# A decoder layer on one core: running sum folded to 64 rows, three places reordered, last stores in halves

## Chip, cores and metric

One core of a Trainium2 chip runs the whole kernel. The metric is device time in microseconds (us) of the execution. The kernel before took 849.17 us in the median of three runs (848.13 to 849.51).

## The reference

One layer of a hybrid causal decoder in fp32, for 512 tokens of width 1024:

```python
h = rms_norm(x, norm_mix)
q_a, k_a, v_a, u_b, gate_b, gate_c, g_a, g_b = split(h @ w_in)
o_a = stick_breaking_attention(heads(q_a), heads(k_a), heads(v_a))   # 8 heads of 64
y_b = gate_b * causal_depthwise_conv(gate_c * u_b, conv_w)           # 3 taps, 512 channels
merged = sigmoid(g_a) * (o_a @ w_branch_a) + sigmoid(g_b) * (y_b @ w_branch_b)
x = x + merged @ w_mix_out
x = x + memory_cross_attention(rms_norm(x, norm_mem_q), rms_norm(mem, norm_mem_kv), ...)  # 256 memory tokens
gate, up = split(rms_norm(x, norm_ffn) @ w_ffn_in)                   # 2816 hidden channels
x = x + (silu(gate) * up) @ w_ffn_out
return rms_norm(x, norm_final)
```

In the stick-breaking attention the weight of key s for query t, with scores z, is

```python
log_fail = where(mask, log_sigmoid(-z), 0)
log_later = cumsum(log_fail, reverse) - log_fail     # the sum over keys between s and t
weights = where(mask, exp(log_sigmoid(z) + log_later), 0)
```

## The kernel before

Activations lie with channels on the 128 partitions and the 512 tokens along the free axis. To hold fp32 precision every operand of a product is kept as two parts, hi (a cast to the matmul's fp32r type, on ScalarE) and lo (the rest, a subtract on VectorE), and a product is three matmuls, hi·hi, lo·hi and hi·lo (`mm3`, L154 to L156). Weights come in tiles of 128x1024, four buffers deep, and are split in the same way (L149, L150).

The stages, by the profiled execution: values of the attention (to 27 us), the stick-breaking stage (27 to 195), branches and merging (to 304), memory keys and values (to 348), the mixing projection with its residual (to 401), memory attention and its output projection (to 508), feed-forward input (508 to 731), feed-forward output (to 840), final norm and stores (to 847).

**The stick-breaking stage.** Four pairs of heads (p = 0 to 3), and in each the four key blocks of 128 keys from the last (kt = 3) to the first (kt = 0): 16 steps. Block kt has 512 − 128·kt queries. For kt of 3 and 2 both heads of a pair share one tile, for 1 and 0 each head has its own. In each step:

- `scores` (L437) makes z in one of four PSUM banks. ScalarE takes |z|, exp and log (L444 to L446), VectorE adds max(z, 0) (L447), GpSimd applies the causal mask (L402). That is e, minus the log of the chance to fail.
- `fails` splits e into the two parts l (L416, L417), and adds the running sum of the later key blocks into e (L462). It is queued in `urgent`.
- `rests` splits this sum into the two parts r (L416, L417 again). It is queued in `behind`, and so runs right after `fails` in the same settling. There are three of them in a pair: the one of kt = 3 is the split l itself, the one of kt = 2 is one 128x512 tile, the ones of kt = 1 are two 128x384 tiles.
- `weights` adds onto z the sum over the keys: a matmul with a matrix of −1 for each part of the rest (L480) and one with a triangle of −1 for each part of l (L483). ScalarE takes exp (a, L485), GpSimd masks (L402), VectorE scales and splits into ah and al (L489, L490).
- `values` multiplies by the values (L502).

Between these steps stand the projections of the coming pair, the convolution (gc L372, cu L378, L379, its taps cv L359, L363, gb L387) and two gates, so that TensorE always has a gemm to run. Here the framework's scheduler places instructions on the engines by the order in which the code issues them and by their dependences. `settle_behind`, called once a step, empties the two queues. At step 9 the factors of the memory's norm go by two GpSimd DMAs to DRAM and back (rmd L534, rmb L536).

**After it.** The merged tiles m = 0 to 7 are split as soon as each is made (mh, ml, L172 and L174); the memory keys km follow (products L154 to L156, eviction L642).

**Feed-forward input.** Seven products for each of 22 blocks m of hidden channels ("forms" i = 0 to 6, L855) in the order of the list `uses`; forms 0, 3, 4 and 5 share PSUM bank z of their block, 2 and 6 bank y. `reads` and `second` take intermediate sums out of the banks: sa on ScalarE (L876), fg and sb on VectorE (L878, L881, L886). The weight forms wf are made six uses ahead (L844, L845). The mean of the norm (acch, accl, L184, L185) is split at use (1,1). The order of TensorE, ScalarE and VectorE is written out by hand in this region and up to the end.

**End.** The last product is made in two halves of 256 columns (`last_half`, p5b L1317). The squares' sum of the last half goes to s1b by ScalarE's accumulator (L1321), VectorE adds it to the other two sums (L1279), ScalarE takes log and exp (L1283, L1284), VectorE corrects (L1293, L1298), and the last two tiles are scaled and stored, 128x512 each, one by the queue of SyncE (SP) and one by that of ScalarE (L1304, L1306, L1309).

Of the kernel before, what the change touches and what calls it, by code (L numbers as in the profile page):

```python
# [13 lines left out]
P = 128  # L14
# [29 lines left out]
def hybrid_layer(ctx: ExitStack, tc: tile.TileContext, xT_d, memT_d, mem_d, cols_d, wv_d, win_d,  # L44
# [28 lines left out]
    def f(ap):  # L73
        return ap.bitcast(F32)
# [224 lines left out]

    urgent, behind = [], []  # L300

    def settle_behind(*last):
        while urgent or behind:
            (urgent or behind).pop(0)(*last)

# [114 lines left out]
    def rests(p, kt, hs, e, w, last):  # L420
        rest[p, kt - 1, hs] = lsplit(e, w, f"r{kt}", 4 // len(hs), last)

# [29 lines left out]
    def fails(p, kt, hs, e, n, last):  # L452
        w = len(hs) * n
        sp[p, kt, hs] = lsplit(e, w, f"l{kt}", 4 // len(hs), last)
        if kt == TT - 1:
            later[hs] = e
            rest[p, kt - 1, hs] = sp[p, kt, hs]
        elif kt > 0:
            t = by_head(e, n)[:, :, P:]
            before = heads_of(kt + 1)[0] if len(heads_of(kt + 1)) == 1 else hs  # L460
            old = by_head(part_of([later[before]], before, hs, n - P)[0], n - P)
            nc.vector.tensor_tensor(out=t, in0=t, in1=old, op=ALU.add)  # L462
            later[hs] = e
            behind.append(lambda *last: rests(p, kt, hs, e, w, last))

# [146 lines left out]
    for m in range(KD):  # L612
# [24 lines left out]
    for m in range(KD):  # L637
# [413 lines left out]
    with tc.manual_schedule(engines={mybir.EngineType.PE, mybir.EngineType.Activation,  # L1051
# [6 lines left out]
        for n, (m, i) in enumerate(uses):  # L1058
# [6 lines left out]
            else:  # L1065
                if i == 1 and m > 0:
                    second(m - 1)
# [206 lines left out]
        def rstd(ts):  # L1274


            a, b = ss[:, :TT][:, ts], ss[:, TT:][:, ts]
            if ts == t1:
                nc.vector.tensor_scalar(out=var[:, ts], in0=b, scalar1=a, scalar2=s1b, op0=ALU.add,  # L1279
                                        op1=ALU.add)  # L1280
            else:
                nc.vector.tensor_tensor(out=var[:, ts], in0=a, in1=b, op=ALU.add)
            after(nc.scalar.activation(ry[:, ts], var[:, ts], AF.Ln, bias=eps_t), tables)  # L1283
# [17 lines left out]
        def store(t, h, how):  # L1301
# [6 lines left out]
            q = nc.scalar if (t, h) == (1, 0) else nc.sync  # L1308
            q.dma_start(out[t * P:(t + 1) * P, h * 512:(h + 1) * 512], y)  # L1309

# [26 lines left out]
        half()  # L1337
        store(0, 0, "act")
        half = last_half(1)
# [70 lines left out]
```

## Time and profile before

| | before |
|---|---|
| median of three runs | 849.17 us (848.13 to 849.51) |
| profiled execution | 848.86 us |
| its span | 847.2 us, granted TensorE clock 0.998 |
| PE (TensorE) busy | 837.0 us, 99% |
| DVE (VectorE) busy | 654.0 us, 77% |
| ACT (ScalarE) busy | 453.3 us, 54% |
| POOL (GpSimd) busy | 158.9 us, 19% |
| DMA | 143.72 MB, mean 170 GB/s |

The profiled execution's own time is 1.7 us above its span, and 0.3 below the median. In a row of a timeline stand the start in us, the busy time, engine, line, operation, out<-in by the program's names without numbers, tile sizes and types, the count if neighbouring instructions are merged into one row, and in brackets the idle time before it with what ended it. Rows of one engine overlap by up to some tenths, since an instruction's drain lies under the next one's start: the pitch from start to start says what an instruction costs its engine. In the table of waits stand the total, the number of waits and the longest. A row of a window has its length, then the busy time and instruction count of each engine, the TensorE clock, the DMA share and GB/s.

### The profile page before, as it was taken

Reading aid. Unit: us, or ns where it says so; the run is one execution under the profiler, and the core shown is the slowest. Engines: PE = TensorE matmul, PEld = TensorE weight load, DVE = VectorE, ACT = ScalarE, POOL = GpSimd, SP = SyncE. Lnnn points to the kernel's source line nnn. Section 1 sums busy time; section 2 is a strip of 40 time slices with the busy share of each in tenths; the row PEclk is TensorE's granted clock in tenths of the full one; section 3 lists DMA queues with packets and bytes.
Section 4 is the critical chain, followed back from the end, with each engine's and each line's share of the span. In section 5 each row is a group of like instructions: output and inputs, shape, how many; then the busy total and the mean of one; then the engine's idle time right before and its main releaser. Section 6 shows DMA issues by size and latency. Waiting matters only on the chain.

```text
span 847.2 us, 12667 instructions
## 1 busy us (share of the span) xinstructions
PE 837.0 (99%) x4779; PEld 737.9 (87%) x4779; DVE 654.0 (77%) x1036; ACT 453.3 (54%) x806; POOL 158.9 (19%) x165
## 2 busy tenths in 40 slices
PE   9999999999999999999999999999999999999996
PEld 7888887888888899888888789999999999988885
DVE  7878978895757686588455689888888778899886
ACT  7576766574333344443444556655555555666654
POOL 0011121220556660163000001111111110000401
PEclk9999999999999999999999999999999999999999
DMA  8552454225588776466431425767767773465552
GB/s 299 158 159 100 131 103 97 80 78 188 195 306 306 268 267 200 171 227 250 152 83 50 111 74 144 177 179 182 191 177 187 190 186 86 149 223 200 179 182 99
DMA packets 51214, 143.72 MB, mean 170 GB/s; under 512 B 5745, under 2 KB 6769, under 8 KB 48338
## 3 DMA queue, kind: packets, MB, share of 16 engines
q1 hardware_dynamic: 41506, 107.89, 38.5%
q0 software_dynamic: 9360, 34.75, 15.7%
q8 instruction: 37, 0.61, 0.3%
q10 hardware_dynamic: 288, 0.28, 0.1%
q14 instruction: 23, 0.19, 0.1%
HBM read 125.20 MB, written 13.64 MB: 164 GB/s over the span
## 4 chain that ended last, share of the span: by engine, by line
PE 95%; DVE 2%; ACT 1%; issue 1%; POOL 0%; POOLq 0%; DVEq 0%; ACTq 0%
PE z L855 15%; PE p L1124 12%; PE y L855 7%; PE pr L154 7%; PE pr L155 7%; PE pr L156 7%; PE v L855 4%; PE r L155 3%; PE r L154 3%; PE r L156 3%; PE v L272 3%; PE mq L156 2%; PE mq L154 2%; PE mq L155 2%; PE br L156 2%; PE br L155 2%
## 5 line engine op out<-in xcount | busy, mean ns | idle before, releaser
L149 ACT CAST wh<-wr 128x1024 fp32r<-128x1024 f32 x84 | 88.0, 1051 | 156.5 <-issue 65.5
L150 DVE TENSOR_TENSOR wl<-wr,wh 128x1024 fp32r<-128x1024 f32 x84 | 112.4, 1340 | 36.5 <-ACT wh L149 35.9
L154 PE MATMUL pr<-xgh,wh 128*128 128x512 f32 x288 | 112.9, 392 | 0.1
L155 PE MATMUL pr<-xgl,wh 128*128 128x512 f32 x288 | 112.4, 390 | 0.0
L156 PE MATMUL pr<-xgh,wl 128*128 128x512 f32 x288 | 112.2, 390 | 0.0
L589 POOL TENSOR_TENSOR pre<-pre 128x512 f32<-128x512 f32 x44 | 73.7, 1679 | 31.7 <-DMA pre<-in_w_ffn_out_dram 29.4
L824 POOL DMA_DIRECT2D ws<-in_w_ffn_in_dram x22 | 26.6, 1210 | 256.1 <-DVE wf L845 120.2
L855 PE MATMUL z<-xdh,wf 128*128 128x256 f32 x352 | 70.4, 283 | 0.0
L156 PEld LDWEIGHTS pr<-xgh,wl 128*128 128x128 f32 x288 | 54.1, 188 | 11.5
L154 PEld LDWEIGHTS pr<-xgh,wh 128*128 128x128 f32 x288 | 54.1, 188 | 10.9 <-DVE gc L372 0.3
L155 PEld LDWEIGHTS pr<-xgl,wh 128*128 128x128 f32 x288 | 54.1, 188 | 10.5
L876 ACT COPY sa<-z 128x256 f32<-128x256 f32 x44 | 16.4, 372 | 79.2 <-PE z L855 79.1
L855 PEld LDWEIGHTS z<-xdh,wf 128*128 128x128 f32 x352 | 58.0, 192 | 0.0
L845 DVE TENSOR_TENSOR wf<-s,wf 128x512 fp32r<-128x512 f32 x44 | 30.3, 690 | 25.9 <-ACT wf L844 25.7
L855 PE MATMUL z<-xdl,wf 128*128 128x256 f32 x176 | 49.8, 283 | 0.0
L936 DVE TENSOR_TENSOR wl<-wr,wh 128x1024 fp32r<-128x1024 f32 x33 | 41.0, 1243 | 4.7 <-ACT wh L1003 4.7
L1003 ACT CAST wh<-wr 128x1024 fp32r<-128x1024 f32 x33 | 34.6, 1049 | 5.5 <-PE xt L1209 2.8
L855 PE MATMUL z<-xch,wf 128*128 128x256 f32 x176 | 35.4, 284 | 0.1
L855 PE MATMUL v<-xoh,wf 128*128 128x256 f32 x176 | 35.4, 283 | 0.0
L855 PE MATMUL y<-xch,wf 128*128 128x256 f32 x176 | 35.4, 283 | 0.0
L855 PE MATMUL z<-xf,wf 128*128 128x256 f32 x264 | 35.4, 283 | 0.0
L855 PE MATMUL y<-xoh,wf 128*128 128x256 f32 x176 | 35.3, 283 | 0.0
(341 smaller groups left out, 2391.8 us busy)
## 6 DMA issues: line engine op xcount, KB each, us to landing
wr<-in_w_in_dram SPq DMA_DIRECT2D x36, 512.0 KB, 3.3
pre<-in_w_ffn_out_dram POOLq DMA_DIRECT2D x11, 1024.0 KB, 8.0
sums<-pre POOLq DMA_DIRECT2D x11, 1024.0 KB, 5.0
ws<-in_w_ffn_in_dram SPq DMA_DIRECT2D x22, 512.0 KB, 3.7
wg<-in_w_ffn_in_dram SPq DMA_DIRECT2D x22, 512.0 KB, 4.3
ws<-in_w_ffn_in_dram POOLq DMA_DIRECT2D x22, 512.0 KB, 6.3
wr<-sums SPq DMA_DIRECT2D x22, 512.0 KB, 3.8
wr<-in_w_ffn_out_dram SPq DMA_DIRECT2D x16, 512.0 KB, 3.8
```

The lines of the kernel that those rows point to most:

```text
L149: after(nc.scalar.copy(h2, raw), lead[-1:])
L150: lows.append(nc.vector.tensor_tensor(out=l2, in0=raw, in1=f(h2), op=ALU.subtract))
L154: nc.tensor.matmul(ps, a[0], b[0], start=start, stop=False, **kw)
L155: nc.tensor.matmul(ps, a[0], b[1], start=False, stop=False, **kw)
L156: nc.tensor.matmul(ps, a[1], b[0], start=False, stop=stop, **kw)
L589: nc.gpsimd.tensor_tensor(out=t[:, a, :], in0=t[:, a, :], in1=t[:, b, :], op=ALU.add)
L824: nc.gpsimd.dma_start(s13, a[:, 0:4:3, :], accum_op=ALU.add)
L845: nc.vector.tensor_tensor(out=w[:, 1, :], in0=raw, in1=f(w[:, 0, :]), op=ALU.subtract)
L855: nc.tensor.matmul(ps[:, :HS], a, b, start=i < 3 and k == 0 and j == 0, stop=k == KP - 1 and j == 2, skip_group_check=True)
L936: nc.vector.tensor_tensor(out=lo, in0=src, in1=f(hi), op=ALU.subtract)
L1003: nc.scalar.copy(hi, raw)
L1124: nc.tensor.matmul(res[i][s2], a[:, ts], b, start=j == 0 and n == 0, stop=n == 2 and j == (BEHIND - 1 if (i, s2) == (5, 1) else NJ - 1))
```

## The change

**1. Running sum.** `rests` no longer makes two parts of 128 rows. ScalarE copies the upper 64 rows of the sum into the lower 64 of a new tile rf, VectorE adds the lower 64 rows, which folds 128 rows into 64. The cast of this goes to the lower half of one operand r (ScalarE), the remainder to its upper half (VectorE). The matmul with −1 sums over all 128 rows, so hi and lo are added in one matmul instead of two. And `rests` goes into a third queue, `unhurried`, that `settle_behind` empties one call later, after that call's `fails`.

**2. Last merged tile.** The split of tile m = 7 (mh, ml) comes after the first memory key's eviction.

**3. Feed-forward entry.** The first uses are (0,3), (1,0), (1,1), (0,4), (1,2), (0,5), (0,6) instead of (0,3), (1,0), (0,4), (1,1), (0,5), (1,2), (0,6). `second(0)` comes at (1,2) instead of (1,1), the split for the mean at (0,4) instead of (1,1), which is the same place in the list.

**4. Last norm.** VectorE adds the first two sums and EPS early (`rstd_begun`); the logarithm reads s1b directly with this as its bias.

**5. Last stores.** The scaling and storing of the last 128 tokens goes by halves of 256 columns: four stores of 128 KB instead of two of 256 KB, three by SyncE's queue and the last by ScalarE's.

The core of the diff:

```diff
     def settle_behind(*last):
-        while urgent or behind:
-            (urgent or behind).pop(0)(*last)
+        some = unhurried[:]
+        unhurried.clear()
+        while urgent or some or behind:
+            (urgent or some or behind).pop(0)(*last)
...
     def rests(p, kt, hs, e, w, last):
-        rest[p, kt - 1, hs] = lsplit(e, w, f"r{kt}", 4 // len(hs), last)
+
+        low, high = HALVES
+        t = tmp("rf")[:, :w]
+        after(nc.scalar.copy(t[low, :], e[high, :]), last)
+        nc.vector.tensor_tensor(out=t[low, :], in0=t[low, :], in1=e[low, :], op=ALU.add)
+        r = lpool.tile([P, w], F32R, tag=f"r{kt}", name=nm("r"), bufs=2 // len(hs))
+        nc.scalar.copy(r[low, :], t[low, :])
+        nc.vector.tensor_tensor(out=r[high, :], in0=t[low, :], in1=f(r[low, :]), op=ALU.subtract)
+        rest[p, kt - 1, hs] = r,
...
-            behind.append(lambda *last: rests(p, kt, hs, e, w, last))
+            unhurried.append(lambda *last: rests(p, kt, hs, e, w, last))
...
-        merged.append(split(sig[0], "m"))
+        if m < KD - 1:
+            merged.append(split(sig[0], "m"))
...
         km.append((hi, lo))
+        if m == 0:
+            merged.append(split(sig[0], "m"))
...
-    uses = [(0, 0), (0, 1), (0, 2)]
-    for m in range(NF):
+    uses = [(0, 0), (0, 1), (0, 2), (0, 3), (1, 0), (1, 1), (0, 4), (1, 2), (0, 5), (0, 6)]
+    for m in range(1, NF):
...
-                if i == 1 and m > 0:
+                if i == (2 if m == 1 else 1) and m > 0:
                     second(m - 1)
...
-            if (m, i) == (1, 1):
+            if (m, i) == (0, 4):
                 mean2 = mean2()
...
+        def rstd_begun(ts):
+            nc.vector.tensor_scalar(out=var[:, ts], in0=ss[:, :TT][:, ts],
+                                    scalar1=ss[:, TT:][:, ts], scalar2=EPS, op0=ALU.add,
+                                    op1=ALU.add)
+        def rstd_of_rest(ts):
+            nc.scalar.activation(ry[:, ts], s1b, AF.Ln, bias=var[:, ts])
+            nc.scalar.activation(ry[:, ts], ry[:, ts], AF.Exp, scale=-0.5)
+            nc.vector.tensor_tensor(out=rv[:, ts], in0=var[:, ts], in1=s1b, op=ALU.add)
...
+        def store_halves(t):
+            r = ra[:, t:t + 1]
+            for c in range(2):
+                cs = slice(c * HS, (c + 1) * HS)
+                for h in (1, 0):
+                    y = ys[t, h][:, cs]
+                    if h:
+                        nc.vector.scalar_tensor_tensor(out=y, in0=y, scalar=r, in1=gain[h][:, cs],
+                                                       op0=ALU.mult, op1=ALU.mult)
+                    else:
+                        nc.scalar.activation(y, y, AF.Copy, scale=r)
+                    q = nc.sync if h or c == 0 else nc.scalar
+                    q.dma_start(out[t * P:(t + 1) * P,
+                                    h * 512 + c * HS:h * 512 + (c + 1) * HS], y)
...
-        rstd(t1)
+        rstd_of_rest(t1)
         rstd_end(t1)
-        store(1, 1, "both")
-        store(1, 0, "act")
+        store_halves(1)
```

TensorE's program goes from 4571 rows to 4555, VectorE's from 1025 to 1036, ScalarE's from 769 to 781. What the change moves on the engines, at the three places that matter most (the line numbers after are those of the changed file, from 2 to 13 above those before):

VectorE (DVE), third head pair, key block 1, before. The names: l split of e, r split of the running sum, cv tap product of the convolution, al second part of the weights.

```order
L417 TENSOR_TENSOR l_1490<-e_1424,l_1489 128x384
L490 SCALAR_TENSOR_TENSOR al_1480<-a_1476,r_372,ah_1479 128x512
L462 TENSOR_TENSOR e_1424<-e_1424,e_1310 128x256
L417 TENSOR_TENSOR l_1495<-e_1430,l_1494 128x384
L359 TENSOR_SCALAR cv_1471<-cu_1467,gcol 128x512
L462 TENSOR_TENSOR e_1430<-e_1430,e_1310 128x256
L363 SCALAR_TENSOR_TENSOR cv_1471<-cu_1467,gcol,cv_1471 128x512
L417 TENSOR_TENSOR r_1503<-e_1424,r_1502 128x384
L363 SCALAR_TENSOR_TENSOR cv_1471<-cu_1467,gcol,cv_1471 128x512
L417 TENSOR_TENSOR r_1507<-e_1430,r_1506 128x384
```

The same place after (rf is the folding add):

```order
L419 TENSOR_TENSOR l_1490<-e_1424,l_1489 128x384
L500 SCALAR_TENSOR_TENSOR al_1480<-a_1476,r_372,ah_1479 128x512
L472 TENSOR_TENSOR e_1424<-e_1424,e_1314 128x256
L419 TENSOR_TENSOR l_1495<-e_1430,l_1494 128x384
L427 TENSOR_TENSOR rf_1499<-rf_1499,e_1314 64x512
L472 TENSOR_TENSOR e_1430<-e_1430,e_1314 128x256
L361 TENSOR_SCALAR cv_1471<-cu_1467,gcol 128x512
L430 TENSOR_TENSOR r_1502<-rf_1499,r_1502 64x512
L365 SCALAR_TENSOR_TENSOR cv_1471<-cu_1467,gcol,cv_1471 128x512 x2
```

The two 128x384 splits r for key block 0 have left this place; the folding of the sum for key block 1 (rf, r_1502) stands in it now, between the second l and the tap products.

TensorE (PE), third head pair, key block 0, before: first head, second head, then the values o of key block 1.

```order
L480 MATMUL z_1529<-r_1502,neg_91 128x384
L480 MATMUL z_1529<-r_1503,neg_91 128x384
L483 MATMUL z_1529<-l_1588,negtri 128x512
L483 MATMUL z_1529<-l_1589,negtri 128x512
L480 MATMUL z_1532<-r_1506,neg_91 128x384
L480 MATMUL z_1532<-r_1507,neg_91 128x384
L483 MATMUL z_1532<-l_1592,negtri 128x512
L483 MATMUL z_1532<-l_1593,negtri 128x512
L502 MATMUL o_1483<-ah_1569,v_339 128x384
L502 MATMUL o_1483<-al_1570,v_339 128x384
L502 MATMUL o_1484<-ah_1580,v_342 128x384
```

After, with xgh, xgl, wh and wl the operands of the next projection:

```order
L512 MATMUL o_1483<-ah_1566,v_339 128x384
L512 MATMUL o_1483<-al_1567,v_339 128x384
L512 MATMUL o_1484<-ah_1576,v_342 128x384
L512 MATMUL o_1484<-al_1577,v_342 128x384
L154 MATMUL pr_1686<-xgh_153,wh_1682 128x512
L155 MATMUL pr_1686<-xgl_154,wh_1682 128x512
L156 MATMUL pr_1686<-xgh_153,wl_1683 128x512
L490 MATMUL z_1527<-r_1595,neg_91 128x384
L493 MATMUL z_1527<-l_1584,negtri 128x512
L493 MATMUL z_1527<-l_1585,negtri 128x512
L154 MATMUL pr_1686<-xgh_158,wh_1682 128x512
L155 MATMUL pr_1686<-xgl_159,wh_1682 128x512
```

The values stand ahead now, then three matmuls of the next projection, then the first head's z with one matmul for its rest instead of two; the second head's follow a few matmuls further on.

VectorE at the feed-forward's entry, before: wf are weight forms, sb and fg reads of the banks, acch and accl the split for the mean.

```order
L845 TENSOR_TENSOR wf_4901<-wg_4876,wf_4901 128x512
L886 TENSOR_TENSOR sb_4791<-y_4812,sb_4791 128x256
L878 TENSOR_TENSOR fg_4905<-v_4904,sa_4823 128x256
L845 TENSOR_TENSOR wf_4920<-ws_4762,wf_4920 128x512
L184 CAST acch_4923<-acc_4373 128x512
L185 TENSOR_TENSOR accl_4924<-acc_4373,acch_4923 128x512
```

After:

```order
L891 TENSOR_TENSOR fg_4897<-v_4896,sa_4831 128x256
L858 TENSOR_TENSOR wf_4911<-wg_4884,wf_4911 128x512
L858 TENSOR_TENSOR wf_4927<-ws_4770,wf_4927 128x512
L184 CAST acch_4930<-acc_4381 128x512
L185 TENSOR_TENSOR accl_4931<-acc_4381,acch_4930 128x512
L899 TENSOR_TENSOR sb_4799<-y_4820,sb_4799 128x256
```

sb, the read that frees bank y of block 0, has moved from ahead of fg and the split for the mean to behind it.

More of the change, by code (lines that the diff above doesn't have):

```diff
@@ L298, in qk_part @@
             settle_behind()
-    urgent, behind = [], []
+    urgent, behind, unhurried = [], [], []
     def settle_behind(*last):
-        while urgent or behind:
-            (urgent or behind).pop(0)(*last)
+        some = unhurried[:]
+        unhurried.clear()
+        while urgent or some or behind:
+            (urgent or some or behind).pop(0)(*last)
     def qk_halves(p, i, t, last):
@@ L1277, in rstd @@
             a, b = ss[:, :TT][:, ts], ss[:, TT:][:, ts]
[L1278 to L1282, printed above, removed]
+            nc.vector.tensor_tensor(out=var[:, ts], in0=a, in1=b, op=ALU.add)
             after(nc.scalar.activation(ry[:, ts], var[:, ts], AF.Ln, bias=eps_t), tables)
@@ L1307, in store @@
                                                op1=ALU.mult)
-            q = nc.scalar if (t, h) == (1, 0) else nc.sync
-            q.dma_start(out[t * P:(t + 1) * P, h * 512:(h + 1) * 512], y)
+            nc.sync.dma_start(out[t * P:(t + 1) * P, h * 512:(h + 1) * 512], y)
+        def store_halves(t):
[12 more added lines that the diff above has]
+                                    h * 512 + c * HS:h * 512 + (c + 1) * HS], y)
         def last_half(c):
@@ L1338, in hybrid_layer @@
         store(0, 0, "act")
+        rstd_begun(t1)
         half = last_half(1)
```

## The prediction

> **What bounds the kernel now.** I read the page first, then the table of what TensorE (PE) waited for, then the timelines of PE and VectorE (DVE) around each wait, then the windows of a few stretches. The first line of the page and two rows of the waits:
>
> ```profile
> PE 837.0 (99%) x4779; PEld 737.9 (87%) x4779; DVE 654.0 (77%) x1036; ACT 453.3 (54%) x806; POOL 158.9 (19%) x165
> PE z L437 <- ACT a L485: 0.9, 1, 0.9
> PE km L154 <- DVE km L642: 0.3, 1, 0.3
> ```
>
> PE is busy for 837.0 of 847.2 us, and inside the program it waits in two places only, 0.9 and 0.3 us by the table. So three things can move the time: fewer matmuls, the few waits, and the tail behind the last matmul. The reserve that a new wait eats is DVE's, 77% busy on the average but not in every stage.
>
> The profiled execution took 848.86 us, 0.3 below the median of the runs (849.17). I sum against the execution and add the result to the median. The measurement of this kernel tells about 0.2% (1.7 us) from no change.
>
> **Edit 1, the saving.** A rest that was a hi part and a lo part on 128 rows, two matmuls for each head, becomes one operand, one matmul. PE loses 16 matmuls: 8 of 256 columns (key block 1) and 8 of 384 (key block 0). PE's timeline in the third pair gives the pitch:
>
> ```profile
> 142.46 0.40 PE L480 MATMUL z<-r,neg 128*128 128x256 f32 x2
> 142.70 0.51 PE L483 MATMUL z<-l,negtri 128*128 128x384 f32 x2
> ...
> 146.63 0.39 PE L156 MATMUL pr<-xgh,wl 128*128 128x512 f32 x1
> 147.95 0.66 PE L437 MATMUL z<-qk,qk 128*128 128x128 f32 x4 [0.93 <-ACT a L485]
> ...
> 151.24 0.51 PE L480 MATMUL z<-r,neg 128*128 128x384 f32 x2
> 151.58 0.62 PE L483 MATMUL z<-l,negtri 128*128 128x512 f32 x2
> ```
>
> Two of 256 columns take 142.70 − 142.46 = 0.24, two of 384 take 0.34. So 8 × 0.12 + 8 × 0.17 = **−2.3 us**, all on PE's path.
>
> The old wait lies in the same rows: from 146.63 to 147.95, less one matmul's 0.2, 1.1 us, and if PE comes there later for another reason it goes: **−1.2** with the slow start of the matmul behind it. ScalarE (ACT) must not become later by as much; it loses eight full-width casts there and gets copies and casts of half the rows.
>
> **Edit 1, the cost.** A rest now takes an ACT copy, a DVE add (call it rf), an ACT cast and a DVE subtract (r), and all of this is issued one step later, behind the next step's urgent split, just ahead of the matmul that wants it. r stands in DVE's queue, which runs in order. Behind rf and r wait the gate and convolution products; for r waits PE, and behind that matmul the whole projection gemm. The price of a half-row operation, and what DVE does in the third pair:
>
> ```profile
> 129.07 0.57 POOL L536 DMA_DIRECT2D rmb<-rmd  x1 [6.69 <-DMA rmd<-rm]
> ...
> 130.38 0.68 DVE L511 TENSOR_TENSOR ot<-o,ot 64x512 f32<-64x512 f32 x1
> 130.98 0.47 DVE L490 SCALAR_TENSOR_TENSOR al<-a,r,ah 128x256 fp32r<-128x256 f32 x1
> ...
> 134.48 0.68 DVE L417 TENSOR_TENSOR r<-e,r 128x512 fp32r<-128x512 f32 x1
> ...
> 142.47 0.55 DVE L417 TENSOR_TENSOR l<-e,l 128x384 fp32r<-128x384 f32 x1
> 142.94 0.48 DVE L359 TENSOR_SCALAR cv<-cu,gcol 128x512 f32<-128x512 f32 x1
> 143.34 0.42 DVE L462 TENSOR_TENSOR e<-e,e 128x256 f32<-128x256 f32 x1
> 143.67 0.75 DVE L363 SCALAR_TENSOR_TENSOR cv<-cu,gcol,cv 128x512 f32<-128x512 f32 x1
> 144.34 0.55 DVE L417 TENSOR_TENSOR r<-e,r 128x384 fp32r<-128x384 f32 x1
> ```
> ```profile
> 139.00:144.00 5.00, 5.00 (x28) 4.38 (x28) 5.00 (x10) 2.04 (x6) 0.61 (x1) 1.00 0.44 160
> ```
>
> Halving the rows saves DVE nothing: 64x512 goes on after 0.60 (130.38 to 130.98) and takes 0.68, as 128x512 does at 134.48.
>
> The third pair, key block 1, is the place that decides. POOL sits 6.69 us on the factors' DMA, so the mask that DVE waits for comes after 129.6 and DVE's work here begins at about 130; then it is full (5.00 of 5.00 from 139 to 144). Before, the rest of this block was made at 134.48, long ahead of PE's matmul at 142.46. Now the order is: second l, rf, e, cv, r. The removed r brings second l forward by some 0.5 of its 0.6 (ACT's logarithms hold the rest), to 142.0. Then 0.47 + rf 0.60 + e 0.33 + cv 0.40 + r 0.68 gives 144.5. PE, which so far has saved 1.15 in two pairs and paid 0.8 (next), is there at 142.1: it waits **2.4**.
>
> The other pairs by the same addition, with these rows:
>
> ```profile
> 111.66 0.68 DVE L174 TENSOR_TENSOR yl<-gb,yh 128x512 fp32r<-128x512 f32 x1
> ...
> 113.44 0.51 PE L480 MATMUL z<-r,neg 128*128 128x384 f32 x2
> ...
> 144.80 0.74 DVE L363 SCALAR_TENSOR_TENSOR cv<-cu,gcol,cv 128x512 f32<-128x512 f32 x1
> ...
> 151.89 0.61 DVE L490 SCALAR_TENSOR_TENSOR al<-a,r,ah 128x384 fp32r<-128x384 f32 x1
> 152.42 0.68 DVE L174 TENSOR_TENSOR yl<-gb,yh 128x512 fp32r<-128x512 f32 x1
> ...
> 159.23 0.69 DVE L378 TENSOR_TENSOR cu<-pr,r0b 128x512 f32<-128x512 f32 x1 [1.39 <-PE pr L156]
> ...
> 186.50 0.60 DVE L490 SCALAR_TENSOR_TENSOR al<-a,r,ah 128x384 fp32r<-128x384 f32 x1
> ...
> 187.00 0.51 PE L480 MATMUL z<-r,neg 128*128 128x384 f32 x2
> ```
>
> - First pair: I give it nothing, since nothing is late ahead of it; if that is wrong, the next line's 0.8 bounds it.
> - Second pair, key block 0: two rf (0.47 each, the pitch of a 384-column split), yl 0.60 and r 0.47 from 111.66 end at 113.7; PE would be there at 113.44 − 0.8 = 112.6. That is 1.1 if DVE gains nothing from the splits taken out earlier and 0.3 if it gains their 0.9 less the half it pays; I take **0.8**.
> - Third pair, key block 0: from r's end (144.5) a convolution product (0.67), the rows 144.80 to 151.89 less the second old r (7.09 − 0.47), al 0.53, two rf 0.94, yl 0.60, r 0.47: 154.2. PE, whose matmuls here now stand behind the four value matmuls and three of the next gemm, is there at 153.3: **0.9**. The gap of 1.39 before 159.23 then takes up DVE's lateness.
> - Fourth pair: from 186.50, 0.53 + 0.94 + 0.47 = 188.4, less some 0.5 for two splits taken out earlier; PE at 187.0 + 0.7 of value matmuls: 187.7 against 187.9, **0.3**.
>
> Waits 0.8 + 2.4 + 0.9 + 0.3 = 4.4. Stage: −2.3 − 1.2 + 4.4 = **+0.9**. The ends: −3.5 if no rest is ever late, +3 if DVE's lateness isn't taken up.
>
> **Edit 2, the last merged tile.** DVE and PE at the entry of the memory keys:
>
> ```profile
> 308.50 1.78 DVE L174 TENSOR_TENSOR ml<-g,mh 128x512 fp32r<-128x512 f32 x1
> ...
> 310.13 0.28 PE L156 MATMUL km<-mgh,wl 128*128 128x256 f32 x1
> 310.76 0.36 PE L154 MATMUL km<-mgh,wh 128*128 128x256 f32 x1 [0.34 <-DVE km L642]
> ```
>
> The long ml goes behind km. PE's next start was 0.63 after its last against a pitch of 0.12, and a little more at the one after: **−0.6**. ml is wanted only by the mixing gemm, tens of us later; what stands behind it on DVE are weight splits with four buffers. Uncovered it would cost the same 0.6 back.
>
> **Edit 3, feed-forward entry.** PE and DVE there:
>
> ```profile
> 515.14 0.52 PE L855 MATMUL z<-xf,wf 128*128 128x256 f32 x3
> 515.77 0.39 PE L855 MATMUL z<-xch,wf 128*128 128x256 f32 x1
> ...
> 521.63 0.28 PE L855 MATMUL y<-xoh,wf 128*128 128x256 f32 x1
> ...
> 519.62 0.42 DVE L886 TENSOR_TENSOR sb<-y,sb 128x256 f32<-128x256 f32 x1
> ...
> 521.34 0.69 DVE L185 TENSOR_TENSOR accl<-acc,acch 128x512 fp32r<-128x512 f32 x1
> ```
>
> The third product of form 0 and the first of form 3 share bank z, and PE lost 0.63 − 3 × 0.12 plus a slow start, 0.38, on ACT's copy. With (1,1) put between, this goes: −0.38. But DVE's read sb of the y bank moves from 519.62 to behind accl. accl ends at 521.95 less sb's own 0.33, sb then at 521.95; (0,6), which writes that bank, would start at 521.63 − 0.38 = 521.25. A new wait of 0.7: net **+0.3** (−0.4 if DVE is that much ahead).
>
> **Edits 4 and 5, the tail.** Last engine work, a window of the last stores, and two load groups that move as much in rows of 2 KB and of 1 KB:
>
> ```profile
> 841.04 0.27 DVE L1279 TENSOR_SCALAR rms<-ss,s1b 128x1 f32<-128x1 f32 x1
> 841.34 0.29 ACT L1283 ACTIVATE rms<-rms,eps_t 128x1 f32<-128x1 f32 x1 [0.34 <-DVE rms L1279]
> ```
> ```profile
> 844.00:845.50 1.50, 0.00 (x0) 0.00 (x0) 0.00 (x0) 0.00 (x0) 0.00 (x0) 0.69 0.90 350
> ```
> ```profile
> mk<-in_mem_dram SPq DMA_DIRECT2D x4, 256.0 KB, 3.0
> mk<-in_memT_dram SPq DMA_DIRECT2D x4, 256.0 KB, 3.0
> ```
>
> The add between accumulator and logarithm goes: −0.3. Two half-width scalings cost some 0.1 more than a whole one (two pitches of 0.33, the 256-column add at 143.34, against one of 0.60). Behind the last issue two stores of 256 KB moved together for 1.5 us at 350 GB/s; now the first halves leave some 0.5 earlier and only 256 KB come last, 0.75 less. Rows of 1 KB land as fast as rows of 2 KB here (3.0 and 3.0). Together **−0.9**; ends −0.1 (halves give nothing) and −1.1.
>
> The Trainium skill, page "DMA: Bandwidth & Descriptors", section "Anatomy of one DMA", puts a DMA at about 2 us fixed plus its bytes by 436 GB/s, most of the fixed part a receipt that no halving shortens. By it a last piece smaller by 128 KB would save 0.3 (an estimate from that page) in place of my 0.75, and the whole sum would come out 0.45 higher. The window's 350 GB/s for two stores at once is what speaks for the larger figure here.
>
> **The sum.** +0.9 − 0.6 + 0.3 − 0.9 = −0.3: 848.6 for the profiled execution, **848.9** beside the median. Its own range is 847.3 to 850.8.
>
> **The rivals.**
> - *No rest is late* (0.30). DVE gets ahead wherever PE waits less, and the third pair's rest arrives with at most 0.8 of waiting in all: −2.3 − 1.2 + 0.8 − 0.6 + 0.3 − 0.9 = −3.9, **845.3**. For it: DVE is 77% busy, and l and al depend on matmuls that come earlier too. Against it: 5.00 of 5.00 in 139 to 144, and the 6.69 us on POOL, which nothing in the change shortens.
> - *The lateness is carried* (0.20), on the other side. If DVE's gap before 159.23 is gone, the fourth pair pays like the third, 2.4 + 0.9 in place of 0.3: +3.0, **851.9**. It decides at that gap: 1.39 us of reserve against some 1 to 2 us of added and delayed DVE work.
> - *Halves give nothing* (0.05): each store's time is mostly fixed, the tail is 0.1 better only, and the time is **849.7**. The page's rule above points that way; no row of this trace shows a lone store's fixed part.
> - That the change doesn't do what it says: the order has the 16 matmuls out, so only the waits are open.
>
> **How the numbers follow.** The forecast has 0.45. Faster than 847.5: the first rival and a small part of the forecast's lower end, 0.34. Slower than 850.9: the second rival and a little of the upper end, 0.23. Within: 0.43. The range 845.0 to 852.0 takes in both rivals with their likeliest values; below are the stage's end of −3.5 together with a free entry, above a worse backlog, 0.1 each.
>
> **What would show it.** PE's instructions 16 fewer. In PE's waits a new row, z behind DVE's r (third pair largest, near 2.4), and no z behind ACT's a. No km row; a y row behind sb of some 0.7. Gap on DVE before the convolution product at 159 smaller, not gone. From last engine work to the end 0.7 less. I am wrong if r never shows in the waits (then 845), or if r's wait repeats in the fourth pair (then 852).

## The result and the profile after

The changed kernel takes 851.11 us in the median of 11 runs (850.29 to 851.95), the kernel before 848.85 in 11 runs (847.88 to 850.21): ratio 1.0027, 95% interval 1.0018 to 1.0035. It is slower by 2.3 us where 0.3 less was forecast. The profiled executions say 850.64 and 848.86, 1.8 apart.

The page of the changed kernel and its table of what TensorE waited for:

```profile
PE 836.4 (99%) x4763; PEld 736.2 (87%) x4763; DVE 657.1 (77%) x1049; ACT 460.0 (54%) x819; POOL 154.9 (18%) x165
PE z L490 <- DVE r L430: 3.2, 3, 2.1
PE y L868 <- DVE sb L899: 0.6, 1, 0.6
```

16 matmuls are gone. The two old waits are gone. In their place stand three waits for r, 3.2 us in all and one of them 2.1, and one for sb, as forecast to some tenths. By the timeline the two smaller waits for r are 0.80 in the second pair of heads (at 113.51) and 0.31 in the fourth (at 189.49). DVE is busy 3.1 us longer and ACT 6.7.

PE's timeline in the third pair of heads shows the long wait and what comes behind it:

```profile
141.67 0.39 PE L156 MATMUL pr<-xgh,wl 128*128 128x512 f32 x1
144.13 0.39 PE L490 MATMUL z<-r,neg 128*128 128x256 f32 x1 [2.07 <-DVE r L430]
...
146.16 0.63 PE L154 MATMUL pr<-xgh,wh 128*128 128x512 f32 x1
146.58 0.63 PE L155 MATMUL pr<-xgl,wh 128*128 128x512 f32 x1
...
148.58 0.39 PE L154 MATMUL pr<-xgh,wh 128*128 128x512 f32 x1
148.81 0.40 PE L155 MATMUL pr<-xgl,wh 128*128 128x512 f32 x1
...
154.57 0.34 PE L490 MATMUL z<-r,neg 128*128 128x384 f32 x1
```

From 146.16 a matmul of 512 columns goes on after 0.42 instead of 0.23. Windows of one microsecond, in which the column behind POOL's is the granted TensorE clock, say why:

```profile
144.00:145.00 1.00, 0.87 (x6) 0.87 (x6) 0.93 (x3) 1.00 (x3) 0.00 (x0) 1.00 0.00 0
145.00:146.00 1.00, 1.00 (x6) 1.00 (x6) 1.00 (x2) 1.00 (x3) 0.00 (x0) 0.50 0.00 0
...
147.00:148.00 1.00, 1.00 (x4) 0.79 (x3) 1.00 (x2) 1.00 (x3) 1.00 (x4) 0.50 0.00 0
148.00:149.00 1.00, 1.00 (x5) 0.82 (x4) 1.00 (x3) 0.97 (x3) 0.26 (x1) 0.79 0.00 0
```

The clock is halved from about 145 to 148.4. By these windows that takes 1.7 us of PE's time (3 × 0.5 + 0.21). I had no such term.

The scores in front of and behind this stretch, before and then after, show how late PE is there: −0.56, then +1.61.

```profile
138.83 1.07 PE L437 MATMUL z<-qk,qk 128*128 128x512 f32 x4
159.03 0.64 PE L437 MATMUL z<-qk,qk 128*128 128x256 f32 x4
```
```profile
138.27 1.07 PE L447 MATMUL z<-qk,qk 128*128 128x512 f32 x4
160.64 0.64 PE L447 MATMUL z<-qk,qk 128*128 128x256 f32 x4
```

VectorE's rows, to be read beside the sum of the prediction: second l, rf, r of key block 1; r of key block 0; and the gap that was to take up the lateness.

```profile
141.48 0.55 DVE L419 TENSOR_TENSOR l<-e,l 128x384 fp32r<-128x384 f32 x1
141.95 0.68 DVE L427 TENSOR_TENSOR rf<-rf,e 64x512 f32<-64x512 f32 x1
...
143.39 0.68 DVE L430 TENSOR_TENSOR r<-rf,r 64x512 fp32r<-64x512 f32 x1
...
153.76 0.55 DVE L430 TENSOR_TENSOR r<-rf,r 64x384 fp32r<-64x384 f32 x1
...
160.84 0.69 DVE L380 TENSOR_TENSOR cu<-pr,r0b 128x512 f32<-128x512 f32 x1 [0.77 <-PE pr L156]
```

Where PE stands at the end of the stick-breaking stage and at the entry of the memory values, before:

```profile
194.79 0.39 PE L502 MATMUL o<-ah,v 128*128 128x512 f32 x1
328.11 0.40 PE L154 MATMUL vm<-wh,mgh 128*128 128x512 f32 x1
```

and after:

```profile
196.54 0.39 PE L512 MATMUL o<-ah,v 128*128 128x512 f32 x1
329.29 0.40 PE L154 MATMUL vm<-wh,mgh 128*128 128x512 f32 x1
```

So +1.75 from the stage, then −0.57 at the memory keys. At the feed-forward's entry, after:

```profile
522.72 0.42 DVE L899 TENSOR_TENSOR sb<-y,sb 128x256 f32<-128x256 f32 x1
...
523.20 0.38 PE L868 MATMUL y<-xoh,wf 128*128 128x256 f32 x1 [0.60 <-DVE sb L899]
```

That is the forecast wait. The last product, from the chain that ended last, before and after (start, length):

```profile
836.38 3.57 PE p5b L1317 x30
```
```profile
838.04 3.57 PE p5b L1354 x30
```

It ends 1.66 later. So the entry gave +0.48 (1.66 − 1.75 + 0.57), and the tail, from the end of the last product to the end of the span, gave nothing: 847.2 − 839.95 = 7.25 before, 848.9 − 841.61 = 7.3 after.

### The profile page after: what moved, and what is told of

Read it like the earlier page. It is cut to its first block, busy times and chain, and to the rows that moved or that the text cites. A ratio compares the mean times of both kernels' runs of the same rounds, so it can differ in the third digit from the quotient of the medians.

```text
span 848.9 us, 12671 instructions
## 1 busy us (share of the span) xinstructions
PE 836.4 (99%) x4763; PEld 736.2 (87%) x4763; DVE 657.1 (77%) x1049; ACT 460.0 (54%) x819; POOL 154.9 (18%) x165
## 4 chain that ended last, share of the span: by engine, by line
PE 92%; DVE 4%; ACT 2%; DMA 1%; issue 1%; POOL 0%; ACTq 0%; DVEq 0%
PE z L868 14%; PE p L1137 12%; PE y L868 7%; PE pr L154 6%; PE pr L155 6%; PE pr L156 6%; PE v L868 4%; PE r L155 3%; PE r L156 3%; PE r L154 3%; PE v L272 3%; PE mq L156 2%; PE mq L154 2%; PE mq L155 2%; PE br L155 2%; PE br L154 2%
## 5 line engine op out<-in xcount | busy, mean ns | idle before, releaser
L149 ACT CAST wh<-wr 128x1024 fp32r<-128x1024 f32 x84 | 87.9, 1050 | 152.9 <-issue 67.1
L150 DVE TENSOR_TENSOR wl<-wr,wh 128x1024 fp32r<-128x1024 f32 x84 | 110.0, 1311 | 37.5 <-ACT wh L149 37.5
L949 DVE TENSOR_TENSOR wl<-wr,wh 128x1024 fp32r<-128x1024 f32 x33 | 40.2, 1220 | 4.6 <-ACT wh L1016 4.3
```

Source lines behind the costliest of these rows:

```text
L149: after(nc.scalar.copy(h2, raw), lead[-1:])
L150: lows.append(nc.vector.tensor_tensor(out=l2, in0=raw, in1=f(h2), op=ALU.subtract))
L949: nc.vector.tensor_tensor(out=lo, in0=src, in1=f(hi), op=ALU.subtract)
```

## The experiments

Each kernel was timed beside the kernel before, whose median in the four groups of runs was 848.67 to 848.85. Each median is one of 5 to 11 executions. The scheduler places every kernel anew, so a difference between two kernels holds the changes of order too. Sixteen kernels, in the order of the questions.

**Which part of the change costs.** First the first edit alone, on the kernel before.

> The kernel before with the first edit alone (folded sum, one step later). Theory A: PE's lateness after the stick-breaking stage is that of the changed kernel, +1.7 us, and nothing else changes: 850.6, ratio 1.002. Rival B (most of the loss is the tail and the feed-forward entry): within 0.5 us of before.

851.66 us, ratio 1.0034 (1.0021 to 1.0048). The whole loss and a little more. Then the other four edits, with the split as before:

```diff
-            unhurried.append(lambda *last: rests(p, kt, hs, e, w, last))
+            behind.append(lambda *last: rests(p, kt, hs, e, w, last))
...
-        rest[p, kt - 1, hs] = r,
+        rest[p, kt - 1, hs] = lsplit(e, w, f"r{kt}", 4 // len(hs), last)
```

> The changed kernel with the first edit undone (split of the running sum as before), the other four edits kept. Theory A: -0.6 at the memory keys, +0.5 at the feed-forward entry, +0.1 in the tail: 848.9, ratio 1.000. Rival B: these four carry the loss, 850.5 or more.

849.16, ratio 1.0002 (0.9993 to 1.0011): they are neutral together, as theory A said. Edit 1 has two parts, which I took apart: folding without delay (only the first pair of lines above), and delay without folding (only the second).

> The changed kernel with its folded rests made in the same step as before (queue behind instead of unhurried); all else as changed. Theory A (the rest is asked for before it is made, and the slow clock after the 2.1 us wait is a result of that wait): the waits of z for r (3.2 us in the changed kernel) go, the clock stays at 1.0 from 144 to 149, and the time falls by 1 to 3.5 us against the changed kernel, to 847.5 to 850; a wait for the second l of the third pair of up to 1.5 us can come in their place, since rf and r then stand ahead of it on DVE. Rival B (the folding's extra work on ACT and DVE costs the time wherever it stands): no change against the changed kernel, 851.

850.53, ratio 1.0021 (1.0013 to 1.0030). That is 0.6 less than the changed kernel, within the intervals of the two, so near rival B and short of theory A's 1 to 3.5. No z waits for r any more, but its table of waits has others:

```profile
PE z L447 <- ACT a L495: 1.8, 2, 1.5
...
PE pr L154 <- DVE gc L374: 1.1, 1, 1.1
PE z L493 <- DVE l L419: 0.7, 2, 0.5
```

These waits come to 3.6, where the kernel with the other four edits only has 1.0 for a. The folding's work, moved earlier, makes other things late. The clock stays at 1.00 in this stage, and the time is hardly better for it. My theory A, that the rest is only asked for too early, falls in this form.

> The changed kernel with the running sum split as before (hi and lo on 128 rows, two matmuls), but one step later: the delay without the folding. Theory H (the delay alone makes the rest late): a wait for r in the third pair again, 1 us or more, with the two matmuls more on top: 851 to 853. Theory B (it is the folding's extra work): no such wait, time as the kernel with the other four edits only, 849.2.

849.65, ratio 1.0013 (1.0004 to 1.0021), with waits for r of 0.7 at the most (0.9 in all). Neither expectation holds: the delay alone costs some 0.5 against e3 (0.7 when each is taken against the kernel before in its own group), at the edge of the intervals, and e9 is well below 851. So with four medians:

| | in its own step | one step later |
|---|---|---|
| split as before | 849.16 | 849.65 |
| folded | 850.53 | 851.11 |

Folding costs 1.4, clear of the intervals; the delay 0.5 or 0.6, which they don't resolve; both 1.95. They add, though folding takes 2.3 us of matmuls away. If that saving is counted in full, what folding adds must be worth 3.7, an estimate.

**Halfway is worse.** Only key block 2's rest in its own step, those of key block 1 later:

> The changed kernel with the rest of key block 2 folded in its own step and those of key block 1 one step later. Theory A (the third pair's late rest and the slow clock behind it are some 3.7 us): no wait of z for r over 1 us in the third pair, clock 1.0, 1.5 to 3.5 us less than the changed kernel, 847.6 to 849.6; waits of other kinds (for l, for gc) of up to 1.5 come in their place. Rival B: 0.5 us less at most.

854.45, ratio 1.0066 (1.0052 to 1.0080): the worst of all apart from the next, and against every expectation. DVE's rf and r of block 2 now stand in the third pair's backlog (134.84 and 137.40), and what comes behind them is later. In front of block 0 of this pair PE waits 0.9 for al and then 1.7 for r, and the clock is halved from 155.0 to 158.4. Two more waits for r, 0.7 and 1.0, lie in the second and the fourth pair.

**Whether the half clock comes from the idle time.** 30 small matmuls in front of the one that waits:

```diff
+            if (p, kt, hs) == (2, 1, (0,)):
+                for _ in range(30):
+                    nc.tensor.matmul(bank[:, w:], neg1, neg1, start=False, stop=False,
+                                     skip_group_check=True)
```

> The changed kernel with 30 matmuls of 128 columns (1.8 us) put in front of the third pair's matmul that waits 2.1 us for r; they write 128 unused columns of its bank. The wait for r ends at the same time. Theory E (the half clock from 145 to 148.4 comes from the idle time before it): TensorE's clock is 1.0 in 144 to 149, and the time is 1.5 us less than the changed kernel's, 849.6. Rival F (the half clock comes from something else, the load there or its date): clock 0.5 as before, time the same or later, 851.1 to 851.5. The scheduler puts key block 0's matmuls ahead of the values here, which adds up to 0.9 of waiting for the rest and takes from either.

855.09, ratio 1.0067 (1.0055 to 1.0080). The windows of three microseconds, with PE's busy time and the clock:

```profile
143.00:146.00 3.00, 3.00 (x27) 1.00 0.00 0
146.00:149.00 3.00, 3.00 (x18) 1.00 0.00 0
...
152.00:155.00 3.00, 1.04 (x5) 1.00 0.11 45
155.00:158.00 3.00, 2.86 (x10) 0.66 0.03 5
```

With the wait filled the clock stays at 1.00 up to 155: theory E is right on the clock. But the time doesn't fall; the small matmuls took 3.3 us, not 1.8, and PE waits at key block 0 for its r, 2.1 us from about 153 on, and the clock halves behind that wait. So the second half of the expectation is wrong. How much the half clock costs can't be read from this kernel: its filler is longer than the wait that it fills, and the scheduler has put key block 0 ahead of the four value matmuls and three of the gemm, 1.4 us sooner, as the expectation warned. The changed kernel's own rows give an estimate: without the 1.7 us PE would be at key block 0 at 154.57 − 1.7 = 152.9, and r ends there at 154.31. So 1.4 of the 1.7 would be a wait for the next rest instead. The executions of the changed kernel point the same way: nine with a mean clock of 0.995 or 0.996 took 850.29 to 851.57, the two with 0.997 and 0.998 took 851.78 and 851.95.

**Whether GpSimd's stand is behind it.** DVE's backlog begins where GpSimd stands 6.6 us on the factors' second DMA in front of a mask. In the changed kernel:

```profile
128.74 0.57 POOL L546 DMA_DIRECT2D rmb<-rmd  x1 [6.60 <-DMA rmd<-rm]
...
129.78 0.35 DVE L499 TENSOR_SCALAR ah<-a,r 128x256 fp32r<-128x256 f32 x1 [5.94 <-POOL a L404]
```

Issuing this load after the stage in the code:

```diff
-        nc.gpsimd.dma_start(rmb, d.broadcast_to([P, MEM]))
-        return rm, rmb
+        return rm, d
...
+    nc.gpsimd.dma_start(rmb, rmd.broadcast_to([P, MEM]))
     stick.close()
```

> The changed kernel with the second of GpSimd's two DMAs for the memory factors (rmb) issued only after the stick-breaking stage, so that GpSimd doesn't stand 6.6 us on it in front of the causal mask. Theory D (the backlog on DVE after that stand is what makes the third pair's rest late, and the clock at 0.5 follows from the wait): DVE's gap before 130 shrinks from 5.9 to about 1 us, the wait for r in the third pair goes from 2.1 to under 0.5, the clock stays at 1.0, and the time falls by some 3.5 us, to 847.5. Rival B (the folding costs its work wherever it stands): under 1 us less, 850.5.

> The kernel before with the same late load and nothing else. Theory D: its waits at 135.5 and 146.6 (1.4 us) go: 847.4, and the changed kernel with the late load is within 0.5 us of it or better, since 16 matmuls less are then worth 2.3. Rival B: within 0.5 of before, and better than the changed kernel with the late load by 2.

851.25 and 848.88, ratios 1.0028 (1.0017 to 1.0038) and 0.9999 (0.9991 to 1.0008): nothing, because nothing moved. In the trace of e5 GpSimd still issues the load at 129.46, after 6.76 us of waiting: the scheduler puts it where it is ready. So the load was tied behind the last product of the weights (`after(..., als[-1:])`):

> As the late load before, with the load of rmb now tied behind the last product of the stick-breaking stage, so that GpSimd's masks really run ahead of it. Theory D (GpSimd's 6.6 us on this DMA make the backlog, and it makes the third pair's rest late): DVE's 5.9 us gap before 130 goes, the wait for r in the third pair goes from 2.1 to under 0.5, the clock stays 1.0, 847.5. Rival B (the work the folding adds is too much wherever it stands): DVE is later than PE all the same, 850 or more.

849.12, ratio 1.0002 (0.9994 to 1.0011), 2.0 less than the changed kernel. DVE's rows there, beside the table of waits, show the backlog gone: the mask comes at once and DVE waits for PE instead.

```profile
124.11 0.35 DVE L499 TENSOR_SCALAR ah<-a,r 128x256 fp32r<-128x256 f32 x1 [0.30 <-POOL a L404]
...
134.55 0.69 DVE L380 TENSOR_TENSOR cu<-pr,r0b 128x512 f32<-128x512 f32 x1 [2.31 <-PE pr L156]
...
141.19 0.69 DVE L430 TENSOR_TENSOR r<-rf,r 64x512 fp32r<-64x512 f32 x1
```
```profile
PE z L490 <- DVE r L430: 2.3, 3, 1.3
```

The third pair's 2.1 us for key block 1 are gone, the clock stays at 1.00. But PE now waits 1.3 at key block 0: less gain than theory D's 3.5, more than rival B allows.

> The kernel before with the same forced late load. Theory D: its waits at 135.5 and 146.6 shrink from 1.4 us to a few tenths: 847.7; the changed kernel with it is then 0 to 0.5 faster. Rival B: the changed kernel with it stays 2 us slower than this one.

847.35, ratio 0.9986 (0.9977 to 0.9995): 1.3 faster than before. The wait at 146.6 that the expectation names (0.9 by the table of before) is gone; the 0.3 at the memory keys stays. So the changed kernel with the forced late load is still 1.8 slower than the kernel before with it, as rival B said. The stand costs both kernels: 2.0 in the changed one, 1.3 in the one before. Of the loss of 2.3 between them it explains some 0.5, no more than the intervals.

**Folding and delay without the backlog.** Four kernels with the forced late load, and with the split for the mean moved behind sb at the feed-forward's entry:

```diff
-            if (m, i) == (0, 4):
+            if (m, i) == (1, 2):
                 mean2 = mean2()
```

This last edit was first tried on the kernel with the untied load, which equals the changed one:

> The changed kernel with the late load, and at the feed-forward's entry the split for the mean made after the read sb (at use (1,2)). Theory D and the reading that sb stands behind accl: the wait of y for sb (0.6 by the table, 0.77 by the pitch) goes, 0.7 less than the changed kernel with the late load alone: 846.8. Rival G (another instruction is late there, the gain is lost behind it): no change against it.

850.65, ratio 1.0021 (1.0012 to 1.0031), 0.6 less than e5; the wait of y for sb is gone from its table.

> The changed kernel with the first edit undone, the load of rmb after the stick-breaking stage, and the mean's split behind the read sb. By the parts measured: 1.3 from the load (kernel before with it), 0.5 to 0.6 at the memory keys, 0.3 at the feed-forward's entry, nothing in the tail: 846.5, the fastest so far. If the gains don't add, 847.3.

> As the kernel above, with the running sum folded, in its own step (no delay). Theory I (the folding costs only where DVE is full; without the backlog the 2.3 us of matmuls remain as a gain): 844.5 to 846. Theory B (the second half-row operation on DVE and the longer chain cost more than the matmuls save everywhere): 847 to 848.5, with waits of PE for DVE's l, gc or g.

> As the kernel with the folded sum in its own step, but one step later (the whole first edit). Theory H (the delay costs by itself): the waits for r at 112 (0.95), 150 (1.4) and 187 (0.4) stay, 848.5 to 849.1. Theory I: within 0.5 of the one without delay.

All three have the forced late load and the mean's split behind sb:

| kernel | median | ratio to before |
|---|---|---|
| split, in its own step (e13) | 847.06 | 0.9977 (0.9968 to 0.9986) |
| folded, in its own step (e14) | 845.69 | 0.9965 (0.9951 to 0.9978) |
| folded, one step later (e16) | 848.24 | 0.9992 (0.9983 to 1.0001) |

Now folding gains 1.4 where it lost 1.4 before, and the delay costs 2.55. The intervals of e13 and e14 just overlap; those of e14 and e16 don't overlap. PE's waits inside e14:

```profile
PE z L493 <- DVE l L419: 0.7, 2, 0.5
```

In e16 the row of z behind r is that of the changed kernel with the forced late load, shown above: 2.3 in three waits, 1.3 the longest. Theory I holds for the folding, theory H for the delay: these three waits are most of the 2.55. e14 beats both kernels, by 3.2 us against before.

> As the folded kernel without delay, with the folding add on GpSimd in place of DVE. Theory B with DVE's work as the cost: 0.5 to 2 us less than with the add on DVE. Rival J (the chain's length, copy, add, cast, subtract on three engines, is the cost, or the masks come later behind the add): the same or slower, since GpSimd's add takes longer.

846.89 (846.42 to 848.79), ratio 0.9981 (0.9973 to 0.9990): slower than e14 by 1.2, as rival J has it, with intervals that just overlap: GpSimd's add is longer (1.54 for 64x512), and the rows of PE below show l late. The eleven runs fall into two groups by the clock: seven with 0.997 or 0.998 at 846.42 to 847.00, four with 0.996 at 848.33 to 848.79. In the profiled one, from the second group, PE waits 1.1 and 0.2 for l in the fourth pair, and the clock falls behind that:

```profile
186.31 0.50 PE L493 MATMUL z<-l,negtri 128*128 128x512 f32 x1 [1.09 <-DVE l L419]
...
187.44 0.50 PE L493 MATMUL z<-l,negtri 128*128 128x512 f32 x1 [0.22 <-DVE l L419]
```
```profile
186.00:189.00 3.00, 2.47 (x9) 2.00 (x10) 3.00 (x5) 2.52 (x5) 0.53 (x2) 0.85 0.02 5
189.00:192.00 3.00, 3.00 (x10) 2.35 (x9) 2.96 (x6) 2.61 (x4) 0.80 (x2) 0.59 0.70 150
```

In these two windows the half clock takes 1.7 us of PE's time (3 × 0.15 + 3 × 0.41). No further rest is waited for behind it, and the two groups lie some 1.8 apart. So here it costs in full.

**The stores.** The last two stores whole again, the last norm as changed:

> The changed kernel with the last two stores whole (fifth edit undone), the last norm as changed. Theory A (a store's time from issue to receipt hardly depends on its size, and three issues in a row on SP make the last one later): the last issue comes 0.6 earlier and lands 0.2 later, so 0.4 us less than the changed kernel, 850.7. Rival C (the prediction's: the bytes behind the last issue count): 0.6 to 0.75 us more, 851.8.

851.52 (850.90 to 851.92), ratio 1.0032 (1.0020 to 1.0045). The difference to the changed kernel, 0.4, is smaller than the intervals. The traces decide more. The changed kernel's last issues, and its last half microseconds with data moving:

```profile
842.69 0.29 ACT L1307 ACTIVATE rms<-s1b,rms 128x1 f32<-128x1 f32 x1
...
844.27 0.33 SPq L1345 DMA_DIRECT2D out_dram<-u  x1
...
844.70 0.37 SPq L1345 DMA_DIRECT2D out_dram<-l  x1
845.17 0.40 SPq L1345 DMA_DIRECT2D out_dram<-u  x1
```
```profile
846.00:846.50 0.50, 0.00 (x0) 0.00 (x0) 0.00 (x0) 0.00 (x0) 0.00 (x0) 0.50 0.99 340
846.50:847.00 0.50, 0.00 (x0) 0.00 (x0) 0.00 (x0) 0.00 (x0) 0.00 (x0) 0.50 0.53 184
```

With whole stores the last product ends 0.25 later, at 841.86, the last issue is at 844.76, and the data end just after 847:

```profile
844.76 0.38 ACTq L1332 DMA_DIRECT2D out_dram<-l  x1
```
```profile
846.50:847.00 0.50, 0.00 (x0) 0.00 (x0) 0.00 (x0) 0.00 (x0) 0.00 (x0) 0.50 0.95 365
847.00:847.50 0.50, 0.00 (x0) 0.00 (x0) 0.00 (x0) 0.00 (x0) 0.00 (x0) 0.50 0.05 12
```

In the kernel before, whose last product ended at 839.95, the data end at about 845.4:

```profile
844.50:845.00 0.50, 0.00 (x0) 0.00 (x0) 0.00 (x0) 0.00 (x0) 0.00 (x0) 0.58 0.99 389
845.00:845.50 0.50, 0.00 (x0) 0.00 (x0) 0.00 (x0) 0.00 (x0) 0.00 (x0) 0.50 0.81 303
```

ACT's store goes out at 844.69, so the last of the four is SP's third. From the last product to the last issue: 845.17 − 841.61 = 3.56 with halves, 844.76 − 841.86 = 2.90 whole. The three stores on SP go out 0.43 and 0.47 after one another, so the last comes 0.66 later. And with the DMA engines full, halves, in rows of 1 KB, move at 340 GB/s, whole stores, in rows of 2 KB, at 389. So the data end 5.2 after the last product either way: what the halves gain by starting sooner they lose in being issued and moved. Before, it was 5.5; the 0.3 between is the add that edit 4 takes out. But the program doesn't end sooner by it: the span ends 1.8 after the data before (845.4 to 847.2) and 2.1 to 2.2 after them with either kind of store (846.8 to 848.9, 847.0 to 849.2). Both tails end 7.3 after the last product (848.9 − 841.61, 849.2 − 841.86). Theory A's direction for the time (0.4 less) isn't borne out, nor rival C's 0.75 more.

## Why the prediction was wrong, point by point

The forecast was a sum of terms that nearly cancel, −0.3, and it came out +1.8 in the profiled executions.

- **Bound.** Right: only PE's path, its waits and the tail moved the time.
- **Matmuls saved and old waits.** Right: 16 fewer, both rows gone.
- **Waits for r.** The mechanism and the places were right: 0.80 in the second pair, 2.07 in the third and 0.31 in the fourth, where I had 0.8, 2.4 and 0.3. Key block 1 of the third pair: 2.07 by the table, 2.4 forecast; the second l started 0.5 earlier than the 142.0 of my sum (141.48) and r ended at 144.07 instead of 144.5.
- **Key block 0 of the third pair, 0.9.** It isn't there as a wait. PE came to it later, at 154.57 instead of 153.3, because the half clock had used up the time; r, forecast for 154.2 (the terms as written give 154.3), ended at 154.3. In e7, where the clock stays up until then, there is a wait for this r, 2.1, in a changed order.
- **Stage, +0.9.** Measured +1.75. The step that failed here is the price of key block 0 of the third pair: 0.9 in my sum, and what stood there was the half clock's 1.7, for which I had no term. Without it PE would have waited some 1.4 by the estimate above, also more than 0.9. By PE's lateness: up to the scores at 138.27 it was 0.2 less than my terms (−0.56 against 0.8 − 1.15). From there to the scores at 160.64 the third pair added 1.61 + 0.56 = 2.2, where my terms give 1.5 (2.4 + 0.9 − 1.2 − 0.24 − 0.34). The difference is 0.8 more at key block 0, 0.3 less at key block 1, and 0.2 that I can't place. The fourth pair added 0.1 (1.61 to 1.75), where my terms give −0.3, with a wait that came out right; where this 0.4 comes from is open. The end I gave, +3, held it all.
- **Memory keys, −0.6.** −0.57.
- **Feed-forward's entry, +0.3.** +0.48, the wait for sb as worked out.
- **Tail, −0.9.** The step that failed most: about 0. Its larger term, the 0.75 for the halves, held the last issue to be no later and rows of 1 KB to be as fast as rows of 2 KB. The last issue comes 0.66 later than with whole stores, from the queue, the rows move at 340 instead of 389 GB/s, and the data end at the same 5.2 after the last product. Its smaller term did come: the logarithm starts 842.69 − 841.61 = 1.08 after the last product, before 841.34 − 839.95 = 1.39, and the data end 0.3 sooner. But the program didn't end sooner by it; what the closing steps wait for isn't settled. From the last engine work to the end there were 4.0 before (842.41 + 0.75 to 847.2) and 4.2 after (843.76 + 0.91 to 848.9), where I had 0.7 less as a sign. The rule of the Trainium skill that I weighed there ("DMA: Bandwidth & Descriptors", section "Anatomy of one DMA": about 2 us fixed in each DMA, a fit for DMAs that GpSimd issues, while these stores go by the queues of SP and ACT) gave 0.3 as an estimate. It was nearer to the nothing measured than my price.
- **Rivals.** The slower one was near in time but had the wrong place: DVE's gap shrank from 1.39 to 0.77 but held, and the fourth pair didn't pay like the third. *Halves give nothing*, to which I gave 0.05, came true for the tail. The sign came out by three misses in one direction, the tail's 0.9, the stage's 0.85 and the entry's 0.2, each inside or close to the ends I had given it; either of the first two alone turns −0.3 into a loss. I gave a time above 850.9 a chance of 0.23.
- What I hadn't seen is that the two parts of edit 1 pull apart: the folding is worth having if DVE has room (1.4 gained in e14 against e13), the delay in no comparison (0.5 to 2.55 lost). I had priced them only together.

The cause of the loss is shown as far as this: the first edit carries it (e2 against e3). GpSimd's stand on a DMA costs the changed kernel 2.0, but the kernel before 1.3 as well, so it doesn't make the loss; it changes which part of the edit pays. With the stand the folding costs 1.4 and the delay about 0.5; without it the folding gains 1.4 and the delay costs 2.55, so that the whole edit still loses some 1.2 (e16 against e13). How the 3.7 that the folding adds with the backlog divides between DVE's second operation and ACT's copy and cast is open, since the add on GpSimd (e15) changed the chain too.

## What to carry to other kernels

A saving on the engine that bounds is bought with work on the one that feeds it: price that work in the window where the feeder is full, not by its average, and look first for what filled that window (here another queue's DMA standing in front of a mask). Change the date of a step and its work apart from each other; delaying a step to just before its consumer leaves nothing to absorb the next delay. Halved stores at the end of this program paid in issues on their queue and in slower rows what they gained by starting sooner.

## What the runs showed of the hardware

- A wait of TensorE of about 2 us is followed by half its clock. In the six kernels with a wait of 2.07 to 2.29 us (the changed one, e2, e4, e5, e7, e8) the clock was 0.50 for 3.4 us, from 0.3 to 1.3 us after the restart (145.0 to 148.4 here, the restart at 144.13). A wait of 1.68 in e12, with 0.69 and 0.26 shortly ahead of it, was followed by the same 3.4 us, from about the restart on. Waits of 1.3 to 1.5 by the table in e1, e10 and e16 were not; one of 1.1 followed by 0.2 in e15 was, by the mean clock in four executions of eleven. The Trainium skill, page "TensorE: Matmul & The Clock Gate", section "Part 1: The HAM clock gate", names an activity window of about 3.4 us that runs freely. The length of the slow stretch agrees, and a free-running window fits that one kernel shows both. It puts the halving behind a whole idle window, though; here a wait of 2.1 us was enough, and the measurement decides.
- The half clock costs no time that the runs show where the next operand is late anyway (the changed kernel: 850.29 to 851.57 with it, 851.78 and 851.95 without, by the mean clock) and some 1.8 us where nothing is (e15).
- Halving an operation's rows saves DVE nothing: rf on 64x512 takes 0.68, as the split of 128x512 did.
- The last stores, with the DMA engines full, moved at 340 GB/s in rows of 1 KB and at 389 in rows of 2 KB; stores issued one after the other on SP's queue went out 0.43 and 0.47 us apart.
- A DMA written later in the code is issued where it is ready, since the scheduler places it: only a tie to a late instruction moved it (e5 against e10).
